# Holding back the context's gathered expert rows while the latents' pairs are selected and their weight table is built

## Chip, core and metric

The kernel runs on one core of one Trainium2 chip. The metric is device time in microseconds (us). All inputs lie in HBM when the kernel starts, and the whole computation, both layers of it, is one program on that core.

## What is computed

The reference runs two layers over 512 latent tokens and 256 context tokens, each a vector of 1024 numbers. A layer is a mixer (differential attention, a chunked MLP, a Fourier mix, gated and merged) and after it a retrieval of experts (PEER): each token picks 16 expert pairs in each of 8 heads, 128 experts in all, out of 16384.

```python
for l in range(DEPTH):                      # DEPTH = 2
    h = modulate(rmsnorm(x, norm1_g[l]), ...)          # latents
    hc = modulate(rmsnorm(xc, norm1_g[l]), ...)        # context
    ...
    x = x + mod[:, 2] * mixer_merge(...)    # attention reads kc, vc of hc too
...
def peer_ffn(h, w_q, sub_keys, u_tab, v_tab):
    ...
        q = rms_unit((t @ w_q).reshape(T, PEER_HEADS, 2, PEER_HALF))
        s = jnp.einsum('thpc,hpkc->thpk', q, sub_keys).astype(F32)
        s1, i1 = lax.top_k(s[:, :, 0], PEER_TOPK)
        s2, i2 = lax.top_k(s[:, :, 1], PEER_TOPK)
        ...
        top_s, pos = lax.top_k(cand_s, PEER_TOPK)
        idx = jnp.take_along_axis(cand_i, pos, axis=-1)
        g = jax.nn.softmax(top_s, axis=-1)
        act = jax.nn.gelu(jnp.einsum('td,thkd->thk', t, u_tab[idx]).astype(F32), approximate=False)
        return jnp.einsum('thk,thkd->td', (g * act).astype(t.dtype), v_tab[idx])
```

The context goes through the experts in the first layer only: in the second it gives keys and values to the attention, and nothing of it is written out. So what the context's experts add in layer 0 is needed at the start of layer 1, where the keys and values of the context are projected.

## The kernel before

**Two ways through the experts.** The latents of layer 0 (all four blocks of 128 tokens) go through every expert: `dense_u` multiplies 128 tiles of the table u with the tokens, `dense_v` multiplies the activations by a routing weight and then by 128 tiles of the table v. The weight is zero for an expert that a token didn't pick; the table of these weights is made by `gtable` (for each token one-hot rows `oa` and `ob`, and a matmul of the two into `px`, copied to `stg` and stored), from the indices `i1x`, `i2x` that `route2` selects (its one-hot masks are `oh`). The two context blocks of layer 0, `rc[0]` and `rc[1]`, go the other way: for each of a token's 128 experts, GpSimd issues an indirect DMA that gathers one u row for each of the 128 tokens (a tile `row` of 128x1024, 512 KB), and VectorE multiplies it with the token and sums up (L867); then the same with the v rows, each scaled and added to `acc` (L876). That is 128 u and 128 v rows for each block, 512 for the two. In layer 1 the last block of the latents goes that way too, with 256 rows.

**Who sets when rows are issued.** Rows have no place of their own in the program. Each group of three matmuls calls `pace()`, which adds the columns over 2.4 (nanoseconds of TensorE) to `owed`; at each 1700 of it, `step()` is called once. One step issues a gather and, LAG = 3 rows behind, uses a row that was gathered earlier. There are LAG + 1 = 4 row buffers, so a gather waits until the row four places ahead of it has been used. Each weight tile that is loaded takes 1800 off `owed` (`spend()`). The VectorE and GpSimd instructions thus stand between those of whatever work has called `pace()`. Queues run in the order written, on each engine.

**The order of the work.** Layer 0: mixer; routing of the context (its rows are queued then); norm and routing of the latents (`route1`, `route2`) and their weight table, with 54 of the 128 tiles of `dense_u` between as filling; then the dense stage, `dense_v` for each tile with the other tiles of `dense_u` between. Layer 1 begins with the Fourier mix and chunk MLP of the latents (`mix()`). Beside it runs `context()`: it waits for the sum of `rc[1]` or for the end of `mix()`, whichever comes first, then finishes the rows that are left one behind the other (`finish`, with no pacing), adds them to the context (`residual`: load `racc`, transpose in `tl`, L898 into `rx`, store `cfin`), and makes the normed context hH, hL (`norm`, L335), which the projections of the context in `qkv` need.

```python
            def context():
                while "summed" not in rc[1] and not mixed:
                    yield
                self.finish(rc[1])
                ...
                    for b, r in enumerate(rc):
                        self.residual(tmp, l - 1, self.cm, cin, b, r["accd"], 1)
                        yield
                    yield from self.norm(tmp, l, cin, CTX, 0, 1, ctx.parts)
```

Of the kernel before, what the change touches and what calls it, by code (L numbers as in the profile page):

```python
# [77 lines left out]
class Ker:  # L78
    def __init__(self, tc, a, es):
        self.tc, self.nc, self.a, self.es = tc, tc.nc, a, es  # L80
        self.uid, self.turn, self.banks = 0, False, PBANKS
        self.wp = self.wb = self.wr = None
        self.jobs, self.flight, self.owed, self.every = [], [], 0, STEPS[0][0]


    def pool(self, es, name, bufs=1, space=None, side=None):
# [738 lines left out]
        self.jobs.append({"l": l, "r": r, "tab": tab, "next": 0})  # L825

    def pace(self, cols):
        self.owed += cols / 2.4
        while self.owed >= self.every:
            self.owed -= self.every  # L830
            self.step()
# [167 lines left out]
    def layer(self, l, xin, cin, xfin, rin):  # L999
        nc, a, tc, two = self.nc, self.a, self.tc, self.two  # L1000
        last = l == DEPTH - 1
# [181 lines left out]
        def ahead(n):  # L1183
            while len(gSs) < n:
                c = order[len(gSs)]
                gSs[c] = self.dense_u(l, c, self.pp, up, dH, dL, "ps", self.banks["ps"])
                yield
        with ExitStack() as e:
            rp = self.pool(e, f"rp{l}")
            for b in range(4):  # L1190
                for n in ("i1", "i2", "g"):
                    if n not in rx[b]:
                        rx[b][n] = rp.tile([P, P], F32, name=f"{n}x{l}_{b}")
            gt, normed = [], []

            def routing():
                with ExitStack() as e2:
                    tmp = self.pool(e2, f"rn{l}")
                    yield from self.norm(tmp, l, xm, SEQ, 1, 0, lambda k: (dH[:, k, :], dL[:, k, :]), r1)
                    normed.append(True)  # L1200
                with ExitStack() as e2:
                    tmp = self.pool(e2, f"rt{l}")
                    yield from self.route1(l, tmp, rp, SimpleNamespace(H=dH, L=dL, T=SEQ), (tmp, *PQB))
                with ExitStack() as e2:
                    tmp = self.pool(e2, f"nat{l}")
                    for b in range(NDB, 4):
                        self.natural(tmp, rx[b]["hnd"], dH, dL, b)
                gt.append(self.pool(e, f"gt{l}"))
                yield from self.route2(gt[0], list(range(NDB, 4)) + list(range(NDB)), rx, l)

            def table():
                for b in range(NDB):
                    while "done" not in rx[b]:
                        yield
                    yield from self.gtable(gt[0], b, rx[b], gd)

            def fill():
                while not normed:
                    yield
                yield from ahead(SPILL[l][0] + NGS - LEAD)  # L1220
            self.interleave((self.ada(*((l, range(10, 12)) if last else (l + 1, range(ADA))), None, "fl"), 4 * AN[l]),
                            (None if last else cr, CR2), (routing(), 1), (table(), 1), (fill(), FILL[l]))
        epp.close()

# [181 lines left out]
```

## Time and profile before

| what | us |
|---|---|
| runs | 4987.19, 4993.69, 11380.49; median 4993.69 |
| profiled execution, its own time | 4982.3 |
| span of its instructions | 4980.5 |
| PE (TensorE) busy | 4521.8 (91%) |
| DVE (VectorE) busy | 3366.8 (68%) |
| POOL (GpSimd) busy | 2029.4 (41%) |
| ACT (ScalarE) busy | 1910.4 (38%) |

The stages as they lie in the span: mixer of layer 0 to about 980; routing of the context and norm of the latents to about 1240; the latents' pair selection and weight table to about 1690; the dense stage from about 1760 to 2893; the mix of layer 1 from about 2920 to 3150; after it projections and attention to about 3700, then routing and table of layer 1 to about 4113, and its dense stage to the end. Busy times of engines lie beside one another; what counts for the time is which engine others wait for in a stage. The run of 11380.49 is a disturbed one.

### The profile page before, as it was taken

The numbers are of one execution on the slowest core, as the hardware profiler recorded it, in microseconds if no ns is written. First come the engines' busy times: TensorE is split into PE (matmuls) and PEld (weight loads), VectorE is DVE, ScalarE is ACT, GpSimd is POOL, SyncE is SP. The second block draws the span as 40 slices with busy tenths as digits, with TensorE's granted clock in tenths as the row PEclk, the third lists the DMA queues.
The fourth block names the chain that finished last, engine by engine and source line by source line (L and its number), as shares of the span: only waits on it lengthen the run. The fifth ranks groups of instructions, "written<-read, shape, count | busy, mean of one in ns | idle before, by whom it ended". The sixth has DMA issues, their size and how long they took to land.

```text
span 4980.5 us, 65298 instructions
## 1 busy us (share of the span) xinstructions
PE 4521.8 (91%) x23501; PEld 3851.7 (77%) x23501; DVE 3366.8 (68%) x6818; ACT 1910.4 (38%) x3201; POOL 2029.4 (41%) x1246
## 2 busy tenths in 40 slices
PE   7899988789789899999899989989897899999998
PEld 4787777667667788877778767767787788999998
DVE  3115485868888667766777874457459976777787
ACT  2222444322578522222222233334334783333332
POOL 1011012335655565655556420111225665555531
PEclk9999999989999999999999999999999899999999
DMA  4442245556567889988889886333536668888986
GB/s 167 144 135 68 92 134 167 170 174 217 200 223 247 297 285 318 318 290 273 272 294 303 306 267 204 101 96 110 170 92 192 214 241 297 293 289 301 302 287 228
DMA packets 447508, 1092.84 MB, mean 219 GB/s; under 512 B 37200, under 2 KB 193744, under 8 KB 440016
## 3 DMA queue, kind: packets, MB, share of 16 engines
q1 hardware_dynamic: 336592, 685.97, 42.2%
q0 software_dynamic: 110592, 402.70, 23.6%
q8 instruction: 185, 3.03, 0.2%
q14 instruction: 139, 1.14, 0.1%
HBM read 970.04 MB, written 118.49 MB: 219 GB/s over the span
## 4 chain that ended last, share of the span: by engine, by line
PE 57%; DVE 15%; issue 8%; DMA 8%; POOL 5%; ACT 4%; SPq 0%; POOLq 0%; DVEq 0%; ACTq 0%
PE du L113 6%; PE du L115 5%; PE du L114 5%; PE da L114 5%; PE da L113 5%; PE da L115 5%; PE ps L113 3%; PE ps L114 3%; PE ps L115 3%; DMA row<-in_u_dram,idxc 2%; POOL row L848 2%; PE px L929 2%; DVE row L867 2%; PE px L113 2%; PE px L115 2%
## 5 line engine op out<-in xcount | busy, mean ns | idle before, releaser
L109 POOL TENSOR_TENSOR wL<-wraw,wH 128x1024 fp32r<-128x1024 f32 x291 | 714.9, 2458 | 1138.9 <-ACT wH L102 1053.4
L102 ACT ACTIVATE wH<-wraw 128x1024 fp32r<-128x1024 f32 x460 | 486.7, 1059 | 1155.2 <-PE du L114 319.5
L113 PE MATMUL du<-dH,wH 128*128 128x512 f32 (+1 forms) x2048 | 781.5, 382 | 64.5 <-DVE da L990 45.5
L115 PE MATMUL du<-dH,wL 128*128 128x512 f32 (+1 forms) x2048 | 774.1, 378 | 43.8 <-DVE wL L109 22.6
L114 PE MATMUL du<-dL,wH 128*128 128x512 f32 (+1 forms) x2048 | 769.5, 376 | 6.5 <-DVE dL L335 6.5
L113 PE MATMUL da<-AH,vH 128*128 128x512 f32 (+1 forms) x1792 | 647.3, 363 | 7.8 <-ACT AH L102 7.8
L114 PE MATMUL da<-AL,vH 128*128 128x512 f32 (+1 forms) x1792 | 651.1, 363 | 0.7 <-DVE AL L109 0.6
L115 PE MATMUL da<-AH,vL 128*128 128x512 f32 (+1 forms) x1792 | 650.5, 363 | 0.0
L867 DVE SCALAR_TENSOR_TENSOR row<-row,hn 128x1024 f32<-128x1024 f32 x384 | 508.6, 1345 | 103.6 <-DMA row<-in_u_dram,idxc 89.8
L102 ACT ACTIVATE vH<-vr 128x1024 fp32r<-128x1024 f32 x256 | 271.7, 1062 | 779.6 <-PE da L114 550.1
L876 DVE SCALAR_TENSOR_TENSOR acc<-row,dots,acc 128x1024 f32<-128x1024 f32 x381 | 501.2, 1315 | 7.6 <-DMA row<-in_v_dram,idxc 3.7
L113 PEld LDWEIGHTS du<-dH,wH 128*128 128x128 f32 x2048 | 399.9, 195 | 123.1 <-DVE da L990 56.2
L848 POOL DMA_INDIRECT row<-in_v_dram,idxc x256 | 327.8, 1280 | 406.1 <-DVE acc L876 354.7
L115 PEld LDWEIGHTS du<-dH,wL 128*128 128x128 f32 x2048 | 400.2, 195 | 94.2 <-DVE wL L109 27.1
L848 POOL DMA_INDIRECT row<-in_u_dram,idxc x256 | 334.2, 1305 | 324.1 <-DVE row L867 228.4
L114 PEld LDWEIGHTS du<-dL,wH 128*128 128x128 f32 x2048 | 400.0, 195 | 47.5 <-DVE dL L335 9.0
L109 DVE TENSOR_TENSOR wL<-wraw,wH 128x1024 fp32r<-128x1024 f32 x169 | 220.8, 1307 | 269.0 <-ACT wH L102 256.4
L990 DVE TENSOR_TENSOR da<-d,da 128x512 f32<-128x512 f32 (+1 forms) x254 | 158.1, 622 | 333.3 <-PE d L115 332.8
L113 PEld LDWEIGHTS da<-AH,vH 128*128 128x128 f32 x1792 | 337.8, 189 | 43.9 <-ACT AH L102 8.5
L114 PEld LDWEIGHTS da<-AL,vH 128*128 128x128 f32 x1792 | 338.0, 189 | 37.7 <-DVE AL L109 2.4
L115 PEld LDWEIGHTS da<-AH,vL 128*128 128x128 f32 x1792 | 338.0, 189 | 35.3
L109 DVE TENSOR_TENSOR vL<-vr,vH 128x1024 fp32r<-128x1024 f32 x256 | 326.2, 1274 | 50.9 <-ACT vH L102 49.2
(385 smaller groups left out, 9441.9 us busy)
## 6 DMA issues: line engine op xcount, KB each, us to landing
wraw<-in_uT_dram SPq DMA_DIRECT2D x256, 512.0 KB, 4.6
vr<-in_v_dram SPq DMA_DIRECT2D x256, 512.0 KB, 6.1
wraw<-in_wt_dram SPq DMA_DIRECT2D x204, 512.0 KB, 3.7
gd<-stg SPq DMA_DIRECT2D x56, 1024.0 KB, 5.4
araw<-in_wada_dram SPq DMA_DIRECT2D x96, 512.0 KB, 4.4
gt<-gd SPq DMA_DIRECT2D x16, 2048.0 KB, 18.0
gt<-gd SPq DMA_DIRECT2D x16, 1536.0 KB, 12.4
gatex<-g SPq DMA_DIRECT2D x48, 256.0 KB, 2.1
```

The lines of the kernel that those rows point to most:

```text
L102: nc.scalar.activation(H, src, AF.Copy)
L109: e.tensor_tensor(L, src, H.bitcast(F32), op=ALU.subtract)
L113: nc.tensor.matmul(out, aH, bH, start=start, stop=False)
L114: nc.tensor.matmul(out, aH, bL, start=False, stop=False)
L115: nc.tensor.matmul(out, aL, bH, start=False, stop=stop)
L848: nc.gpsimd.indirect_dma_start(out=row, out_offset=None, in_=self.a[f"{job['tab']}{job['l']}"], in_offset=bass.IndirectOffsetOnAxis(ap=r[" ...
L867: nc.vector.scalar_tensor_tensor(row, row, 1.0, job["hn"], op0=ALU.mult, op1=ALU.mult, accum_out=dots[:, j:j + 1])
L876: nc.vector.scalar_tensor_tensor(job["acc"], row, dots[:, j:j + 1], job["acc"], op0=ALU.mult, op1=ALU.add)
L929: nc.tensor.matmul(gp[:, j * P:(j + 1) * P], ob[:, j, :], oa[:, j, :], start=True, stop=True)
L990: add = nc.vector.tensor_tensor(acc7, s[:, :TD], acc7, op=ALU.add)
```

## The change

A flag `held` makes `pace()` do nothing. It is set ahead of the latents' pair selection in layer 0 and taken back when the weight table has been built. In between, `owed` doesn't grow and no `step()` is called: no row is issued and none is used. No work is taken away; the rows that don't stand there stand later. `STEPS`, `LAG` and all else are as before, and layer 1 sets no flag.

```diff
@@ Ker.__init__
         self.jobs, self.flight, self.owed, self.every = [], [], 0, STEPS[0][0]
+        self.held = False
@@ Ker.pace
     def pace(self, cols):
+        if self.held:
+            return
         self.owed += cols / 2.4
         while self.owed >= self.every:
@@ Ker.layer, routing() and table()
                         self.natural(tmp, rx[b]["hnd"], dH, dL, b)
+                self.held = not last
                 gt.append(self.pool(e, f"gt{l}"))
                 yield from self.route2(gt[0], list(range(NDB, 4)) + list(range(NDB)), rx, l)
@@
                     yield from self.gtable(gt[0], b, rx[b], gd)
+                self.held = False
```

Three lines are put in ahead of most of the code, so L867, L876, L848, L897 and L898 of the kernel before are L870, L879, L851, L900 and L901 of the changed one.

GpSimd's queue in the table stage, the kernel before (`row<-in_u_dram` are the gathers, `oh` the masks of the pair selection, `ob` the one-hot rows of the table, `wL` the low part of a dense weight tile):

```order
L848 DMA row_11468<-in_u_dram,idxc_0_94 128x1024
L926 TENSOR_SCALAR ob_11526<-iota,sT_10796 128x128
L848 DMA row_11585<-in_u_dram,idxc_0_94 128x1024
L786 TENSOR_TENSOR oh_11490<-oh_11490,pIF_10906 128x2048
L926 TENSOR_SCALAR ob_11598<-iota,sT_10796 128x128
L926 TENSOR_SCALAR ob_11627<-iota,sT_10796 128x128
L848 DMA row_11677<-in_u_dram,idxc_0_94 128x1024
L786 TENSOR_TENSOR oh_11591<-oh_11591,pIF_10906 128x2048
```

The same queue in the changed kernel, from the last gather ahead of the stage on:

```order
L851 DMA row_14252<-in_u_dram,idxc_0_94 128x1024
L110 TENSOR_TENSOR wL_10592<-wraw_10589,wH_10591 128x1024
L110 TENSOR_TENSOR wL_10680<-wraw_10677,wH_10679 128x1024
L787 TENSOR_TENSOR oh_10673<-oh_10673,pIF_10413 128x2048
L787 TENSOR_TENSOR oh_10718<-oh_10718,pIF_10413 128x2048
L110 TENSOR_TENSOR wL_10832<-wraw_10829,wH_10831 128x1024
L749 CAST pIF_10870<-pI_8762 128x256
L929 TENSOR_SCALAR ob_10772<-iota,sT_10766 128x128
```

The gathers are gone from between the masks and the one-hot rows. Counted over the two orders on VectorE, 104 rows have been used at the first multiplication of the dense stage in the kernel before, and 41 in the changed one: 63 rows stand later.

VectorE's queue at the end of the context's rows in the mix of layer 1, the kernel before (`pq` is Fourier work, `acc` the sum of the context's v rows, `rx` the residual):

```order
L876 SCALAR_TENSOR_TENSOR acc_20735<-row_24142,dots_17818,acc_20735 128x1024
L876 SCALAR_TENSOR_TENSOR acc_20735<-row_24158,dots_17818,acc_20735 128x1024
L109 TENSOR_TENSOR wL_24432<-wraw_24429,wH_24431 128x1024
L109 TENSOR_TENSOR pq_24013<-ps_24154,pq_24012 128x256
L109 TENSOR_TENSOR pq_24015<-ps_24182,pq_24014 128x256
L109 TENSOR_TENSOR wL_24518<-wraw_24515,wH_24517 128x1024
L109 TENSOR_TENSOR pq_24015<-ps_24235,pq_24014 128x256
L898 SCALAR_TENSOR_TENSOR rx_24256<-tl_24258,mod_72,rx_24256 128x128 x2
```

The same queue in the changed kernel, from the last two instructions of the chunk MLP (`ct`) on:

```order
L641 SCALAR_TENSOR_TENSOR ct_24717<-tl_24712,sm_76,cbs_24270 128x512
L645 TENSOR_TENSOR ct_24717<-ct_24717,cu_24532 128x512
L879 SCALAR_TENSOR_TENSOR acc_21944<-row_24655,dots_19024,acc_21944 128x1024
L879 SCALAR_TENSOR_TENSOR acc_21944<-row_24693,dots_19024,acc_21944 128x1024
L879 SCALAR_TENSOR_TENSOR acc_21944<-row_24705,dots_19024,acc_21944 128x1024
...
L879 SCALAR_TENSOR_TENSOR acc_21944<-row_24809,dots_19024,acc_21944 128x1024
L879 SCALAR_TENSOR_TENSOR acc_21944<-row_24812,dots_19024,acc_21944 128x1024
L901 SCALAR_TENSOR_TENSOR rx_24825<-tl_24827,mod_72,rx_24825 128x128 x4
L901 SCALAR_TENSOR_TENSOR rx_24825<-tl_24836,mod_72,rx_24825 128x128 x4
```

Before, the last row stands in the middle of the Fourier mix, and mix work follows it. Now 34 rows stand in one piece behind the whole mix (with one small instruction of the projections among them), and the residual behind these. Between the last dense tile of layer 0 and the end of the chunk MLP stand 54 rows, where 25 stood in all.

TensorE's queue at the same place, the kernel before (`tl` with `ident` are the transposes of the residual, `ps` Fourier products):

```order
L115 MATMUL ps_24235<-bH_24172,z_23494 128x256
L897 MATMUL tl_24258<-ident,racc_24254 128x128
L113 MATMUL ps_24277<-bH_24172,z_23493 128x256
L114 MATMUL ps_24277<-bL_24173,z_23493 128x256
L115 MATMUL ps_24277<-bH_24172,z_23494 128x256
```

And in the changed kernel (`ps_25012` is the end of a projection of the latents, `tl` the residual, L294 and L305 the norm of the context, `px_25013` its projection):

```order
L115 MATMUL ps_25012<-wL_25060,hH_22991 128x512
L116 MATMUL ps_25012<-wH_25059,hL_22992 128x512
L900 MATMUL tl_24827<-ident,racc_24823 128x128 x4
L900 MATMUL tl_24836<-ident,racc_24823 128x128 x4
L900 MATMUL tl_24850<-ident,racc_24846 128x128 x4
L900 MATMUL tl_24859<-ident,racc_24846 128x128 x4
L294 MATMUL tl_24908<-onescol,nr_24869 128x1 x2
L305 MATMUL tl_24930<-dg_24927,ones 128x128 x2
L114 MATMUL px_25013<-wH_25017,hH_22993 128x512
```

Before, the transposes stand between Fourier products of the mix. Now residual, norm and the first projection of the context stand in one piece, behind the last product of the chunk MLP and 44 matmuls of a latent projection, with nothing between.

## Rows read from the trace of the kernel before

**Rows 1.** The page, part 1: busy time of each engine.

```profile
PE 4521.8 (91%) x23501; PEld 3851.7 (77%) x23501; DVE 3366.8 (68%) x6818; ACT 1910.4 (38%) x3201; POOL 2029.4 (41%) x1246
```

**Rows 2.** Stretch, length; PE, PEld, DVE, ACT, POOL busy; clock, DMA share, GB/s.

```profile
1240.00:1680.00 440.00, 377.48 (x2071) 297.56 (x2070) 378.76 (x883) 314.07 (x612) 256.92 (x152) 0.95 0.67 230
1800.00:2100.00 300.00, 300.00 (x1325) 248.40 (x1324) 224.88 (x237) 86.51 (x111) 181.66 (x127) 1.00 0.92 314
2200.00:2500.00 300.00, 272.20 (x1154) 219.64 (x1153) 209.22 (x296) 77.10 (x96) 167.65 (x108) 0.98 0.83 272
2900.00:2920.00 20.00, 3.27 (x14) 3.22 (x15) 14.24 (x31) 2.52 (x4) 6.04 (x5) 0.58 0.84 289
2920.00:3140.00 220.00, 207.62 (x1089) 164.14 (x1088) 109.23 (x183) 77.33 (x121) 16.27 (x15) 0.96 0.65 211
```

**Rows 3.** What TensorE waited for in the table stage: us, times, longest.

```profile
PE tl L906 <- DVE i2x L787: 14.7, 2, 9.7
PE px L929 <- DVE ob L926: 8.5, 7, 2.1
PE du L115 <- DVE wL L109: 7.6, 3, 6.3
...
PE du L115 <- POOL wL L109: 7.0, 4, 3.8
```

**Rows 4.** The row instructions of the table stage: duration ns min/median/max.

```profile
L867 DVE SCALAR_TENSOR_TENSOR row<-row,hn x59: 1204/1216/3385, 1240.7 to 1679.1; 128x1024 f32<-128x1024 f32 x59
L848 POOL DMA_INDIRECT row<-in_u_dram,idxc x58: 937/1284/1931, 1242.2 to 1672.7; - x58
```

**Rows 5.** The chain of waits through the table stage, shares by line.

```profile
by line: issue 12.6%; PE px L929 10.7%; DVE ob L926 7.6%; PE du L115 7.2%; ACT stg L930 7.0%; PE du L113 6.8%; PE du L114 6.7%; DVE oa L918 5.2%; DVE row L867 4.3%; POOL oh L786 4.2%; POOL ob L926 3.2%; POOL wL L109 2.9%; ACT ob L924 2.9%; 
```

**Rows 6.** The dense stage, 2200 to 2500, u rows: waits, and the rows themselves.

```profile
PE du L113 <- DVE da L990: 25.8, 12, 4.6
...
DVE row L867 <- DMA row<-in_u_dram,idxc: 36.2, 19, 5.1
...
L867 DVE SCALAR_TENSOR_TENSOR row<-row,hn x90: 1207/1219/3503, 2200.4 to 2499.1; 128x1024 f32<-128x1024 f32 x90
```

**Rows 7.** VectorE in time at the end of the context's rows: start, length.

```profile
3033.36 1.28 DVE L876 SCALAR_TENSOR_TENSOR acc<-row,dots,acc 128x1024 f32<-128x1024 f32 x1 [0.59 <-DMA row<-in_v_dram,idxc]
3035.69 1.34 DVE L876 SCALAR_TENSOR_TENSOR acc<-row,dots,acc 128x1024 f32<-128x1024 f32 x1 [1.04 <-DMA row<-in_v_dram,idxc]
...
3038.37 1.28 DVE L876 SCALAR_TENSOR_TENSOR acc<-row,dots,acc 128x1024 f32<-128x1024 f32 x1 [1.02 <-DMA row<-in_v_dram,idxc]
...
3040.71 2.60 DVE L876 SCALAR_TENSOR_TENSOR acc<-row,dots,acc 128x1024 f32<-128x1024 f32 x2
```

**Rows 8.** GpSimd in time at the same place: three of its last gathers for the context.

```profile
3030.40 1.87 POOL L848 DMA_INDIRECT row<-in_v_dram,idxc  x1 [0.59 <-DVE acc L876]
...
3033.89 1.58 POOL L848 DMA_INDIRECT row<-in_v_dram,idxc  x1 [0.30 <-issue]
3035.77 0.94 POOL L848 DMA_INDIRECT row<-in_v_dram,idxc  x1 [0.30 <-issue]
```

**Rows 9.** From the last row to the normed context: stores and loads, residual, norm.

```profile
3043.34 0.33 SPq L878 DMA_DIRECT2D accdc<-acc  x1
...
L898 DVE SCALAR_TENSOR_TENSOR rx<-tl,mod,rx x16: 347/350/353, 3053.3 to 3066.4; 128x128 f32<-128x128 f32 x16
...
3066.77 0.56 SPq L899 DMA_DIRECT2D cfin<-rx  x1
...
L335 DVE SCALAR_TENSOR_TENSOR hL<-nt,mod,hH x8: 479/484/488, 3094.5 to 3110.5; 128x256 fp32r<-128x256 f32 x8
```

**Rows 10.** Landing of the gathers from 2990 to 3045, beside the mix.

```profile
DMA to landing us min/median/max: 4.4/5.7/8.7
```

**Rows 11.** A row's multiplication in the dense stage, and GpSimd beside it.

```profile
2320.63 3.33 DVE L867 SCALAR_TENSOR_TENSOR row<-row,hn 128x1024 f32<-128x1024 f32 x1 [0.90 <-DMA row<-in_u_dram,idxc]
...
2320.49 2.39 POOL L109 TENSOR_TENSOR wL<-wraw,wH 128x1024 fp32r<-128x1024 f32 x1 [0.77 <-ACT wH L102]
```

## Prediction

> **What bounds the kernel now.** I read the busy times first: TensorE is busy for 91% of the span, VectorE for 68%, GpSimd for 41% [rows 1]. A change that takes no work from TensorE can therefore gain only in stretches where TensorE stands still, and loses wherever it makes a new one. So the second view is the busy time by stretches [rows 2]. The reader is to see how unlike they are. Where v rows of the context run beside the dense stage (1800 to 2100), TensorE has no idle time at all, with the DMA engines at 0.92. Where u rows run there (2200 to 2500), it is idle for 300 - 272.2 = 27.8 us. In the table stage, from which the change takes the rows, it is idle for 440 - 377.5 = 62.5 us, with VectorE busy for 379 of 440. In the mix of layer 1 it is idle for 220 - 207.6 = 12.4 us, and VectorE and the DMA engines have room (109 of 220; 0.65).
>
> Third come the waits of TensorE in the table stage [rows 3]. It waits for VectorE's pair selection (14.7), one-hot rows (8.5) and weight split (7.6): 30.8 us for VectorE, and 7.0 for GpSimd's split. The rows themselves are named in none of these; they stand ahead of what is named, in the same queues. The chain of waits says the same from the other side: VectorE's row multiplications hold 4.3% of those 440 us, 19 us [rows 5].
>
> Last come the end of the context's rows in layer 1 and what follows on it, in order of time [rows 7 to 9], since the order of the changed kernel puts them in another place: the last 34 rows, residual, norm and projection of the context in one piece behind the mix.
>
> **Table stage, a gain.** 63 rows stand elsewhere. The trace has 59 multiplications there at a median of 1.216 us and 58 gathers at 1.284 [rows 4]: VectorE loses 59 x 1.216 = 72 us of its 379, GpSimd 58 x 1.284 = 74 us of its 257. TensorE's work of 377 us stays, so no more than its idle 62.5 us can come back, and not all of that: part of it is start-up of each table matmul and ScalarE's work, which no row delays. Lower bound: the 19 us for which rows hold the chain, less what takes their place there, since one-hot rows and stage copies (7.6% and 7.0%) run close behind [rows 5]; I take 10. Upper bound: 50. Between them I take the waits for VectorE, 31 us, as the row nearest to the question: with a fifth of its work gone, VectorE should be ahead of the table matmuls. **-31** (-50 to -10).
>
> **Dense stage, a loss.** As many u rows more run beside dense tiles, in the same small clusters ahead of the add into `da`. In the stretch with u rows 90 of them go with 27.8 us of idle TensorE, 25.8 of it a wait for that add [rows 2, 6]. 63 x 27.8 / 90 = **+20**. The bounds: 10, if half of those waits would be there without rows; 28, if the first tiles of the stage, which have less slack, take half as much again. In return as many v rows leave the end of the stage, which cost nothing [rows 2].
>
> **The mix of layer 1.** Ahead of the burst 54 rows run where 25 ran. The 29 more of 0.524 MB are 15.2 MB over some 220 us, 69 GB/s on 211: 280, less than the 314 at which TensorE was never idle [rows 2]. On VectorE they are 29 x 1.28 = 37 us [rows 7] in a stretch with 111 free. The context's residual and norm leave the stretch, and can take some of its 12.4 us of idle TensorE along. I take **0** (-6 to +13: all of the context's share, or as much idle again as is there now).
>
> **The burst, a loss.** What hid the last rows and the context's norm was the mix. Now nothing of the mix is left behind them: on TensorE only 44 matmuls of a latent projection stand ahead of the first transpose of the residual. At 300 us / 1325 = 0.226 us each [rows 2] that is 10 us of cover. Rows: four are in their buffers, 4 x 1.28 = 5 us [rows 7]. Each of the other 30 goes round a ring of four buffers: gather, landing, multiplication, next gather. From the start of the gather at 3030.40 to its use at 3035.69, which waited for the landing, it took 5.29 us [rows 7, 8]; with the use of 1.28 and GpSimd's 0.30 ahead of a gather that makes 6.9 us for four rows, 1.7 each. GpSimd alone gave (3035.77 - 3030.40) / 3 = 1.79 for one. 30 x 1.7 = 51, so 56 us in all. Bounds: 1.28 for each of 34, 44 us, if VectorE is the limit; and (3040.71 - 3033.36) / 3 = 2.45 for each, 83 us, which is what uses at the end of the context's rows had, with weight loads and Fourier work between [rows 7].
>
> **What follows on the burst.** The last sum goes out at 3043.34, the first normed tile is there at about 3094.5 + 0.9 = 3095.4 [rows 9]: 52 us, all hidden by the mix so far, of which sixteen residual steps of 0.35 us took 13 because of other work between. With the engines otherwise empty I take 48 (41 to 52). Nobody works meanwhile: TensorE's queue has the residual's transposes, two small norm products and the context's projection there, in this order, and everything of `qkv` and the attention is queued behind them. So 56 + 48 - 10 = **+94** (79 to 125). TensorE comes out of such a stop at a lower granted clock: at the boundary of the layers, busy for 3.27 of 20 us, it had 0.58 (between its two levels) [rows 2]. I put **+3** on the time until it is back (0 to 5).
>
> **What two pages would make of it.** A row's multiplication that ran beside GpSimd's split of a weight tile took 3.33 us where the median is 1.219, and the split 2.39 [rows 6, 11]. The Trainium skill, "SBUF — State Buffer", section "Who interferes with whom", says why: a VectorE instruction with two SBUF inputs and a GpSimd instruction that reads SBUF exclude each other. This trace agrees for this pair. The rule speaks for taking rows out of the table stage and against putting them beside the splits of the dense stage, where rows reach 3.5 us too [rows 4, 6]; both are in the terms above already, so the sum stays.
>
> For the ring of four buffers the landing decides, and rows show 4.4 us at least and 5.7 in the median [rows 10]. The Trainium skill, "DMA: Bandwidth & Descriptors", section "Anatomy of one DMA — SWDGE (gpsimd) path", gives about 2.0 us plus bytes over 436 GB/s, by which an estimate for 512 KB is 3.2 us. By that page VectorE would be the limit at 1.28 us a row, the burst 44 us and the sum 12 us lower. This trace has no gather as quick, so the rows stand.
>
> **The sum.** -31 + 20 + 0 + 94 + 3 = +86 on the profiled execution's 4982.3: 5068. That execution lies 11.4 us below the median of the runs and 4.9 below the lowest of the two that are undisturbed. I add 7 and forecast **5075 us**, 1.6% above the median of 4993.69. About 2% (100 us; slower from 5094, faster below 4894) is what a measurement of this kernel can tell from no change.
>
> **Rivals.**
> 1. *Slower: the burst goes at the pace of 2.45 us a row.* At the end of the mix the weight loads of the projection are fetched ahead, and gathers that share the DMA engines with them land late; the uses at 3033 to 3041 show three waits in a row for a landing [rows 7]. Then the burst is 83 us and the time 5075 + 27 = 5102, +2.2%. It decides from 2.25 us a row (19 us more). Against it: these gaps had other VectorE work between, and in a standstill weight loads stop once their buffers are full.
> 2. *Slower: the table stage gives little back.* The rows filled gaps in queues that wait for TensorE or ScalarE anyway, and the change doesn't free what it means to free. With 10 instead of 31 the time is 5096. For it: rows hold 4.3% of the chain only [rows 5]. Against it: VectorE is at 86% there and is what TensorE waits for most [rows 2, 3].
> 3. *Little loss.* The table stage gives 50, the burst runs at VectorE's pace (44) and what follows takes 41: -50 + 20 + 75 + 3 = +48, 5037; with the dense stage at 10 it is 5027. For it: residual and norm are alone on their engines.
> 4. *Faster by over 2%.* All idle time of the table stage and of the mix together is 75 us [rows 2]; even with no burst that is 1.5%. Nearly excluded.
>
> **How the numbers follow.** The forecast's case, all terms near their middle, between 5040 and 5093: 0.50. Rival 1: 0.22. Rival 2: 0.13. Rival 3: 0.13. Rival 4: 0.02. The forecast and rival 3 are within 2% (0.63); rivals 1 and 2 lie just above the line, so I leave 0.35 for slower and 0.63 for no difference. The range leaves out the lower half of rival 3 and the upper tail of rival 1, when its pace goes together with a small gain in the table stage (5102 + 21 = 5123): 5025 to 5118. All the cases but rival 4 are a loss; whether it passes 2% is nearly open.
>
> **What will show it.** In the table stage of the changed kernel TensorE's busy time stays at about 377 us in some 410, and the waits for VectorE's `ob`, `i2x` and weight splits are mostly gone. In the first tiles of the dense stage u rows run for some 200 us longer, with TensorE waiting for the add into `da`. At about 3150 us (some 10 us earlier if these two terms hold) VectorE has 34 uses of `acc` in a row, 1.7 us apart, waiting for landings, and TensorE is empty for about 94 us, which ends with `px` of the context's projection. Wrong would make it: other projections of TensorE that run ahead of the transposes; rows that pile up in the mix until VectorE holds TensorE there; or a table stage whose waits move to ScalarE's `stg` and ends no earlier.

## Result: 1.7% slower, inside the range

The changed kernel takes 5071.18 us (median of four runs, 5068.46 to 5072.83), the kernel before 4990.98 beside it. The ratio is 1.017 (95% interval 1.0157 to 1.0183), where +1.6% was forecast, and under the 2% drawn as the line for "slower". One run of the kernel before (11380.49 us) is disturbed and left out of the ratio: against the median of the other three, 4988.27, the loss is 83 us, against the median of all four 80.

The busy time of each engine over the span is as before to within 1% [rows 1], since no work was added or taken away; the span is 88 us longer.

```profile
span 5068.8 us, 65325 instructions
...
PE 4532.9 (89%) x23501; PEld 3853.3 (76%) x23501; DVE 3384.8 (67%) x6818; ACT 1910.5 (38%) x3201; POOL 2019.6 (40%) x1246
```

The stretches, as in [rows 2]: the table stage, which ends at 1642 and not at 1673; the last dense tiles and the mix of layer 1; and the 100 us behind the mix.

```profile
1240.00:1640.00 400.00, 363.60 (x2044) 287.45 (x2043) 313.08 (x768) 310.14 (x608) 169.00 (x94) 0.97 0.49 174
2860.00:3140.00 280.00, 247.56 (x1269) 198.93 (x1267) 177.73 (x229) 82.32 (x122) 84.24 (x66) 0.95 0.78 262
3140.00:3240.00 100.00, 8.86 (x22) 3.84 (x20) 49.56 (x64) 3.11 (x8) 36.74 (x31) 0.52 0.62 205
```

In the last of them TensorE works for 9 of 100 us, with a granted clock of 0.52, near the lower of its two levels. That is the loss, and the three longest waits of TensorE from 3100 to 3300 name it:

```profile
PE tl L900 <- DMA racc<-accdc: 63.5, 1, 63.5
PE tl L294 <- DVE nr L283: 17.6, 1, 17.6
PE tl L900 <- DVE rx L901: 8.2, 15, 1.9
```

The first of these is the burst with the store and load of its sum, the second the norm's sums, the third the residual. Ahead of the sum's store VectorE does nothing but rows (and one instruction of 0.22 us); its view in time, as [rows 7], first and last of the burst and two from the middle:

```profile
3133.78 5.24 DVE L879 SCALAR_TENSOR_TENSOR acc<-row,dots,acc 128x1024 f32<-128x1024 f32 x4
3141.16 1.28 DVE L879 SCALAR_TENSOR_TENSOR acc<-row,dots,acc 128x1024 f32<-128x1024 f32 x1 [2.15 <-DMA row<-in_v_dram,idxc]
...
3152.64 1.28 DVE L879 SCALAR_TENSOR_TENSOR acc<-row,dots,acc 128x1024 f32<-128x1024 f32 x1 [0.90 <-DMA row<-in_v_dram,idxc]
...
3196.02 1.35 DVE L879 SCALAR_TENSOR_TENSOR acc<-row,dots,acc 128x1024 f32<-128x1024 f32 x1 [0.31 <-DMA row<-in_v_dram,idxc]
```

34 rows from 3133.78 to 3197.37 are 63.6 us, 1.87 for each. The row instructions of the burst and the landing of its gathers, as [rows 4, 10]:

```profile
L879 DVE SCALAR_TENSOR_TENSOR acc<-row,dots,acc x34: 1280/1285/1627, 3133.8 to 3196.0; 128x1024 f32<-128x1024 f32 x34
...
DMA to landing us min/median/max: 4.6/5.5/6.5
```

A multiplication still takes 1.285 us. The rest goes into the round of gather, landing and use over four buffers: VectorE waits for landings 19 times in the burst, 18.5 us in all, and between its gathers GpSimd waits for a row to be used. No run here changes the number of buffers, so this is read from the waits and not tested. What follows, on TensorE and SyncE, as [rows 9]:

```profile
3139.89 0.39 PE L116 MATMUL ps<-wH,hL 128*128 128x512 f32 x1
3203.73 0.45 PE L900 MATMUL tl<-ident,racc 128*128 128x128 f32 x1 [63.46 <-DMA racc<-accdc]
...
3237.09 1.01 PE L294 MATMUL tl<-onescol,nr 128*128 128x1 f32 x4 [17.64 <-DVE nr L283]
3241.14 1.20 PE L305 MATMUL tl<-dg,ones 128*128 128x128 f32 x4 [3.03 <-DVE dg L299]
3243.86 0.79 PE L114 MATMUL px<-wH,hH 128*128 128x512 f32 x1 [1.53 <-ACT hH L335]
3244.46 0.63 PE L115 MATMUL px<-wL,hH 128*128 128x512 f32 x1
```

```profile
3197.40 0.33 SPq L881 DMA_DIRECT2D accdc<-acc  x1
```

From the store of the sum (3197.40) to the first projection of the context (3243.86) it is 46.5 us. TensorE's last matmul ahead of the stop begins at 3139.89 and ends at about 3140.3, so it stands, but for transposes, for 103.6 us. The gains and losses lie where landmarks of the two traces fall against one another. A landmark is the first or last instruction of a line, and its lag is its time in the changed kernel less that in the kernel before, in us. For the adds into `da` (the sum of the dense stage) it is read from these two lines, the kernel before first:

```profile
L990 DVE TENSOR_TENSOR da<-d,da x127: 678/692/692, 1764.2 to 2896.5; 128x512 f32<-128x512 f32 x127
```

```profile
L993 DVE TENSOR_TENSOR da<-d,da x127: 677/691/692, 1725.1 to 2884.7; 128x512 f32<-128x512 f32 x127
```

| landmark | lag |
|---|---|
| routing of the context, about 960, ahead of the change | +6.0 |
| first transpose of the weight table | +0.8 |
| last `stg` of the weight table | -31.0 |
| first add into `da` | -39.1 |
| last add into `da` | -11.8 |
| first normed latents of layer 1 | -10.3 |
| last chunk MLP product | -15.2 |
| first softmax of layer 1's attention | +88.4 |
| end of the span | +88.3 |

The first 6 us are none of the change: the instructions are the same there, and in the first 100 us this execution had a granted clock of 0.85, the profiled one of the kernel before 0.98. Without them the trace says +82, the runs 80 to 83.

### The profile page after: what moved, and what is told of

Read it like the earlier page. It is cut to its first block, busy times and chain, and to the rows that moved or that the text cites. A ratio compares the mean times of both kernels' runs of the same rounds, so it can differ in the third digit from the quotient of the medians.

```text
span 5068.8 us, 65325 instructions
## 1 busy us (share of the span) xinstructions
PE 4532.9 (89%) x23501; PEld 3853.3 (76%) x23501; DVE 3384.8 (67%) x6818; ACT 1910.5 (38%) x3201; POOL 2019.6 (40%) x1246
## 4 chain that ended last, share of the span: by engine, by line
PE 55%; DVE 16%; DMA 11%; issue 9%; POOL 4%; ACT 3%; SPq 0%; POOLq 0%; DVEq 0%; ACTq 0%
PE du L114 5%; PE du L115 5%; PE du L116 5%; PE da L115 5%; PE da L116 5%; PE da L114 5%; PE ps L114 3%; DMA row<-in_u_dram,idxc 3%; PE ps L116 3%; PE ps L115 3%; POOL row L851 2%; PE px L932 2%; DVE row L870 2%; PE px L114 2%; PE px L116 2%
## 5 line engine op out<-in xcount | busy, mean ns | idle before, releaser
L870 DVE SCALAR_TENSOR_TENSOR row<-row,hn 128x1024 f32<-128x1024 f32 x384 | 516.6, 1365 | 124.2 <-DMA row<-in_u_dram,idxc 112.4
L879 DVE SCALAR_TENSOR_TENSOR acc<-row,dots,acc 128x1024 f32<-128x1024 f32 x381 | 503.0, 1320 | 41.3 <-DMA row<-in_v_dram,idxc 37.3
L851 POOL DMA_INDIRECT row<-in_v_dram,idxc x256 | 328.5, 1283 | 421.6 <-DVE acc L879 366.7
L851 POOL DMA_INDIRECT row<-in_u_dram,idxc x256 | 333.0, 1301 | 322.8 <-DVE row L870 250.2
L114 PEld LDWEIGHTS da<-AH,vH 128*128 128x128 f32 x1792 | 336.8, 188 | 41.1 <-ACT AH L103 6.1
```

Of the source, the lines that this page charges most:

```text
L114: nc.tensor.matmul(out, aH, bH, start=start, stop=False)
L851: nc.gpsimd.indirect_dma_start(out=row, out_offset=None, in_=self.a[f"{job['tab']}{job['l']}"], in_offset=bass.IndirectOffsetOnAxis(ap=r[" ...
L870: nc.vector.scalar_tensor_tensor(row, row, 1.0, job["hn"], op0=ALU.mult, op1=ALU.mult, accum_out=dots[:, j:j + 1])
L879: nc.vector.scalar_tensor_tensor(job["acc"], row, dots[:, j:j + 1], job["acc"], op0=ALU.mult, op1=ALU.add)
```

## Experiments

Ratios are to runs of the kernel before on the same chip, with the 95% interval. Lags are landmarks as in the table, against the same profiled execution of the kernel before. They carry the scatter of both executions: in the run with cover but without the hold, whose instructions up to layer 1 are those of the kernel before, the table stage took 5 us longer than there, and the dense stage 7.

**The stop without the hold.** The flag is set for the last 27 dense tiles instead, where v rows cost TensorE nothing [rows 2].

```diff
-                self.held = not last
                 gt.append(self.pool(e, f"gt{l}"))
...
                 for c in range(NK):
+                    self.held = not last and c >= NK - 27
                     room[0] += not self.spilled(l, c)
...
+                self.held = False
                 known = not last and TD == SEQ
```

> No hold in the table stage; instead pace() is held for the last 27 tiles of the dense stage of layer 0, where v rows cost TensorE nothing. The row count at the start of the dense stage is that of the kernel before (104 used); 32 rows stand in one piece behind the mix of layer 1 (34 in the changed kernel). Theory (the loss is the stop at the end of the mix: burst, then residual and norm with nothing beside them): 32 x 1.87 us, the pace in the changed kernel's burst, + 47 - 10 = 97 us over the kernel before, less up to 10 from fewer rows beside the last dense tiles and the boundary: 5075 to 5090. Rival (the loss comes from the rows that the hold puts into the first dense tiles, and rows behind the mix are hidden somehow): 4985 to 5010.

Measured: 1.0181 (1.0164 to 1.0198), +90 us, within the 87 to 97 of the theory's sum; the median of 5072.98 lies just under its 5075, since the kernel before took 4980.57 beside it. Table and dense stage keep their times (lags -1.2 at the last `stg`, -0.7 at the last add into `da`), and the attention begins 91.9 us late. The waits of TensorE from 3100 to 3300:

```profile
PE tl L900 <- DMA racc<-accdc: 59.1, 1, 59.1
PE tl L294 <- DVE nr L283: 16.5, 1, 16.5
PE tl L900 <- DVE rx L901: 9.5, 15, 3.3
```

They are those of the changed kernel. So the stop alone makes a loss of this size, without the hold in the table stage; the rival falls.

**The table stage alone.** The 63 u rows are left out of the computation.

```diff
                 r["dots"] = gp.tile([P, P], F32, tag="dots", name=self.nm("dots"), bufs=2)
+                nc.vector.memset(r["dots"], 0.0)
...
                 self.held = False
+                if not last:
+                    self.jobs[0]["next"] += 63
```

> As the changed kernel, but the 63 u rows that it puts off are left out altogether (not gathered, not multiplied; their dot products stay zero), so the dense stage and layer 1 carry the same rows as in the kernel before. Theory: the gain of the table stage and of the way into the dense stage, 37 + 8 us in the trace, stays: 4940 to 4955. Rival (what the table stage gains is given back at the start of the dense stage, since TensorE is the limit there anyway): 4970 to 4990.

Measured: 0.9927 (0.9910 to 0.9945), -36 us. Lags: -37.9 at the last `stg`, -43.5 at the first add, -37.7 at the last one, -43.4 at the attention. What the table stage gains is kept to the end.

**Rows caught up in the dense stage, with the hold and without.**

```diff
-STEPS = ((1700, 1700, 1700), (1700, 1700, 1700))
+STEPS = ((1700, 1700, 1460), (1700, 1700, 1700))
```

> As the changed kernel, but the dense stage of layer 0 calls for a row at each 1460 of owed time, not 1700, so that the 63 rows are caught up there: 26 rows stand behind the first dense output add, 25 in the kernel before, and none behind the mix. Theory: gain of the table stage (-45), cost of 63 more u rows in the dense stage (+27), no stop in layer 1, nothing for rows that follow one another more closely beside v tiles: 4965 to 4980, a little faster than before. Rival (a denser row stream, with the DMA engines at 0.92 already, makes TensorE wait in the dense stage): 5000 to 5040.

> The kernel before with only the pace in the dense stage of layer 0 changed to 1460: no hold, and all rows of the context are used before the end of the dense stage. It prices the denser row stream alone. Theory: 4980 to 4995, no change, the rows that cross the boundary now lie a little earlier. Rival (denser rows cost TensorE time): 5010 to 5040.

Measured: 1.0081 (1.0064 to 1.0098) with the hold, 1.0098 (1.0079 to 1.0117) without. Both times (medians 5021.93 and 5026.43) lie in the rivals' ranges: here the theory of an almost free denser stream fell. Between the first and the last add into `da` the kernel before gets 63 us later by the pace alone (-4.9 to +58.1), the one with the hold 83 (-42.3 to +41.1). Why is seen in the v rows from 1800 to 2100. First the stretch at 1460 without the hold, as [rows 2]:

```profile
1800.00:2100.00 300.00, 283.42 (x1211) 230.79 (x1210) 257.74 (x231) 82.74 (x102) 190.98 (x130) 0.98 0.92 317
```

Then the groups of row instructions there (busy us, mean ns, idle time ahead), in that kernel and, in the fence behind it, in the kernel before:

```profile
L876 DVE SCALAR_TENSOR_TENSOR acc<-row,dots,acc 128x1024 f32<-128x1024 f32 x110 | 171.8, 1562 | 22.6 <-DMA row<-in_v_dram,idxc 22.2
```

```profile
L876 DVE SCALAR_TENSOR_TENSOR acc<-row,dots,acc 128x1024 f32<-128x1024 f32 x104 | 133.1, 1280 | 0.3 <-DMA row<-in_v_dram,idxc 0.3
```

And the same rows at 1460 by min/median/max:

```profile
L876 DVE SCALAR_TENSOR_TENSOR acc<-row,dots,acc x110: 1267/1274/3925, 1800.3 to 2098.0; 128x1024 f32<-128x1024 f32 x110
```

Only six more rows were used in these 300 us, but they cost VectorE 39 us more: the mean of a row goes from 1280 to 1562 ns, its median stays, and the longest takes 3925. Besides, VectorE waits 22 us for landings (0.3 before), and TensorE, which had no idle time here, stands for 16.6 us, all but 0.1 of it a wait for the add into `da`. The longest row, and the weight split on GpSimd beside it:

```profile
1874.55 3.92 DVE L876 SCALAR_TENSOR_TENSOR acc<-row,dots,acc 128x1024 f32<-128x1024 f32 x1
...
1874.97 2.41 POOL L109 TENSOR_TENSOR wL<-wraw,wH 128x1024 fp32r<-128x1024 f32 x1
```

In these 300 us 18 of the rows take more than 1.5 us, and each of the 18 overlaps such a split; of the 92 shorter ones one does. At 1700 the rows fell into the gaps between the splits: three of 103 touch one, and none is stretched. By the Trainium skill, "SBUF — State Buffer", section "Who interferes with whom", a VectorE instruction with two SBUF inputs and a GpSimd instruction that reads SBUF contend for a pair of ports that is locked, not shared. The trace agrees: the stretched rows reach about a row's own 1.27 us and a split's 2.4 together.

**Rows paced faster in the mix.** The change with 900, and with 1300, at the start of layer 1.

```diff
-STEPS = ((1700, 1700, 1700), (1700, 1700, 1700))
+STEPS = ((1700, 1700, 1700), (900, 1700, 1700))
```

> As the changed kernel, with the pace at the start of layer 1 raised (a row at each 900 of owed time, not 1700). All 88 rows that are left behind the dense stage then stand among the instructions of the mix, the last of them ahead of the chunk MLP's gating, and none behind the mix; table and dense stage are those of the changed kernel. Theory (the loss of the changed kernel is the stop at the end of the mix, about 97 us, and VectorE has room in the mix): the stop is gone; -41 for table stage and entry, +27 for u rows in the dense stage, and 0 to 30 for rows that the ring of four buffers (1.87 us each) can't deliver in time: 4985 less 14, plus 0 to 30, so 0.995 to 1.004 of the kernel before. Rival, after what a denser stream did to the dense stage (63 rows closer together cost 60 to 80 us there): VectorE's queue holds the mix up by as much, 1.010 to 1.015.

> As the changed kernel, with the pace at the start of layer 1 at 1300: 17 rows stand in one piece behind the mix, half of the 34. Theory (the stop is 1.87 us for each row behind the mix, and 47 for residual and norm, less 10 of cover, whatever stands ahead): 17 x 1.87 = 32 us less than the changed kernel, which was 1.017 to 1.018: 1.010 to 1.012 of the kernel before, with a standstill of TensorE of some 72 us. Rival (the rows that now stand closer together in the mix cost there what the burst saves): 1.016 to 1.020.

Measured: 1.0092 (1.0074 to 1.0109) and 1.0125 (1.0106 to 1.0144), each between the ranges of its theory and its rival. With 900 it is just under the rival's: the long wait for `racc` shrinks to 7.2 us, but the mix is held up. Its stretches:

```profile
2940.00:3060.00 120.00, 113.57 (x658) 90.28 (x656) 71.89 (x84) 38.97 (x64) 43.44 (x35) 0.99 0.89 312
3060.00:3160.00 100.00, 73.65 (x305) 59.20 (x305) 72.38 (x80) 22.98 (x29) 47.00 (x38) 0.88 0.87 303
...
3180.00:3200.00 20.00, 1.63 (x7) 1.57 (x8) 5.57 (x22) 3.33 (x8) 0.00 (x0) 0.53 0.29 92
```

TensorE is idle for 26 of 100 us while rows pile up from 3060, with the DMA engines at 0.87, and still stands for most of 20 us in the norm of the context, which comes so late that little of the mix is left beside it. With 1300 the wait for `racc` falls from 63.5 to 34.5 us, 29 for 17 rows fewer behind the mix, about what 1.87 a row says. But the mix, which got 5 us shorter in the changed kernel, gets 13 longer here (lag -12.8 at the first normed latents, +0.2 at the last chunk MLP product), so 18 us are given back. The theory's mechanism holds, and the mix, for which it had no price, takes more than half of what the burst saves.

**Half of the hold.** Two kernels: the hold until the pair selection has been written out, with the mix at 900; and the hold from there on.

```diff
                 yield from self.route2(gt[0], list(range(NDB, 4)) + list(range(NDB)), rx, l)
+                self.held = False
...
                     yield from self.gtable(gt[0], b, rx[b], gd)
-                self.held = False
```

```diff
-                self.held = not last
                 gt.append(self.pool(e, f"gt{l}"))
                 yield from self.route2(gt[0], list(range(NDB, 4)) + list(range(NDB)), rx, l)
+                self.held = not last
```

> As the run with the mix paced at 900, but the hold ends with the pair selection; beside the rest of the weight table rows run again. 52 rows are put off instead of 63, 77 are left behind the dense stage, none behind the mix. Theory (the rows cost the table stage about 0.65 us each, wherever they stand in it): gain of the table stage 52/63 of 41 = 34, cost in the dense stage 52/63 of 27 = 22, mix 0 to 20: 0.997 to 1.002 of the kernel before. Rival (rows cost most while VectorE is busy without a gap, in the pair selection): the whole 41 stays, 0.994 to 0.998.

> As the changed kernel, but the hold begins when the pair selection has been written out, so 14 rows are put off instead of 63; 39 are left behind the dense stage (25 before), all of them beside the mix, the last one at nearly the same place of the mix as before. Theory: a gain of 14 x 0.65 = 9 us in the table stage, a cost of 14 x 0.34 = 5 in the dense stage, no stop: 0.997 to 1.001 of the kernel before. Rival (the gain of the hold comes from the pair selection alone): 1.000 to 1.003.

Measured: 1.0052 (1.0036 to 1.0069) and 1.0013 (1.0000 to 1.0025). From the first transpose of the table to its last `stg`, the first gains 31 us (-4.1 to -35.5), as much as the whole hold (32); the second loses 3 (+0.8 to +3.6). So the gain of the table stage comes with the rows of the pair selection, as the rival had it, and not evenly from all rows. On the way into the dense stage, from the last `stg` to the first add into `da`, it is the other way round: the first gains nothing (-35.5 to -33.7), the second 8 us (+3.6 to -4.3), as much as the whole hold there.

Why the pair selection? From its first mask product on GpSimd to the last index on VectorE it takes 308 us in the kernel before and 184 in the changed one, of which VectorE is busy for 272 and 179 (the third of the busy times in these stretches, the kernel before first):

```profile
1269.00:1577.00 308.00, 257.76 (x1410) 202.87 (x1409) 272.34 (x636) 223.98 (x441) 191.09 (x109) 0.94 0.63 218
```

```profile
1262.00:1446.00 184.00, 155.89 (x844) 122.40 (x843) 179.09 (x437) 134.53 (x263) 92.21 (x47) 0.93 0.45 160
```

VectorE is busy nearly without a gap only once the rows are gone. Before, it also waited some 20 us for the masks on GpSimd, whose queue had the gathers between them; with the hold 1.8 us of that are left (the kernel before, then the changed one):

```profile
DVE i1x L787 <- POOL oh L786: 10.2, 2, 6.2
DVE i2x L787 <- POOL oh L786: 9.4, 2, 4.8
```

```profile
DVE i2x L788 <- POOL oh L787: 1.8, 1, 1.8
```

Every run here holds back multiplications and gathers together, so how much of the gain belongs to VectorE and how much to GpSimd's queue stays open. As a whole the first run is slower than either expectation, since the mix takes 28 us of it back (-5.4 at the first normed latents, +23.0 at the attention). The second lies in the rival's range, with an interval that reaches into the theory's. With 14 rows put off it lost 22 us in the dense stage of its profiled execution, as much as the first with 52, which no price per row explains; its runs scatter from 4979 to 5003 us, and that stays open.

**Cover for the stop.** The context's projections are written behind those of the latents, with eight weight tiles loaded and split a second time; once with the hold, once without.

```diff
-    self.interleave((self.qkv(tmp, l, both, PE3[l]), 1), (g0 if last else None, 0.6))
+    self.interleave((self.qkv2(tmp, l, both, PE3[l]) if last else self.qkv(tmp, l, both, PE3[l]), 1), (g0 if last else None, 0.6))
...
+    def qkv2(self, tmp, l, ss, e="pool"):
+        yield from self.qkv(tmp, l, ss[:1], e)
+        nc, a, s = self.nc, self.a, ss[1]
+        g = tmp.tile([P, 2, 64], F32, tag="gk", name=self.nm("gk"), bufs=1)
+        nc.sync.dma_start(g, a["kg"][l])
+        acc, = yield from self.projN(l, W_K, ss[1:], e)
+        self.qknorm(tmp, acc, g[:, 0, :], s.lat, *s.k)
+        acc, = yield from self.projN(l, W_V, ss[1:], e)
+        for b, o in enumerate(acc):
+            self.split(s.v[0][:, b, :], s.v[1][:, b, :], o)
+        yield
```

> As the changed kernel, with hold, 88 rows left and 34 of them behind the mix; but in layer 1 the projections of the context (keys, values) are written after all projections of the latents instead of sharing each weight tile with them. Eight weight tiles are loaded and split a second time. On TensorE 236 matmuls now stand between the chunk MLP and the residual's transposes (44 before), and 268 instructions between the first transpose and the first projection of the context (20 before). Theory (the loss is the missing cover, and nothing of the rows' work itself): (236 - 44 + 268 - 20) x 0.226 = 99 us more cover for a stop of about 97 us, so most of it is gone; -41 + 27 remain, and 0 to 20 for the extra loads and for VectorE's split of weights and qk-norm behind rows: 0.997 to 1.002 of the kernel before. Rival (VectorE's and the DMA engines' work for the rows holds up the projections of the latents as well, so cover on TensorE doesn't help): 1.010 to 1.017.

> The kernel before with the same order of projections in layer 1 and no hold: the price of the second load and split of eight weight tiles, and of the other order, alone. Theory: TensorE has the same matmuls, the DMA engines stand at a quarter there: 0.998 to 1.003 of the kernel before. If it is faster than the run with the hold, the hold isn't worth its cost even where the stop is covered; by -41 + 27 the hold should be faster than this by 5 to 25 us.

Measured: 1.0129 (1.0115 to 1.0144) with the hold, 1.0011 (0.9996 to 1.0027) without. The extra loads are about free. With the hold some 20 us come back, of the 75 to 100 that the expectation asked for: the time lies in the rival's range, and the hold is some 55 us slower than the same order without it, where 5 to 25 faster was expected. The two stretches behind the mix, and the longest waits of TensorE from 2880 to 3450 that belong to the second:

```profile
3140.00:3200.00 60.00, 49.98 (x200) 38.97 (x199) 46.76 (x49) 15.16 (x19) 39.74 (x31) 0.91 0.87 310
3200.00:3260.00 60.00, 12.86 (x35) 6.94 (x33) 31.82 (x74) 4.39 (x9) 12.03 (x7) 0.56 0.44 140
```

```profile
PE tl L294 <- DVE nr L283: 16.6, 1, 16.6
PE tl L912 <- DMA racc<-accdc: 14.9, 1, 14.9
...
PE tl L912 <- DVE rx L913: 12.6, 15, 6.4
```

While the burst runs TensorE is busy now (50 of 60 us), so cover does work, and the rival's reason is not what happened; the projections that were counted on for the second half stand behind the residual's transposes and the norm's products in TensorE's queue, and wait with them. Counting instructions between two places was the mistake: what stands behind a waiting instruction covers nothing.

**The two parts of the stop, and the dense stage alone.** Left out of the computation: 30 of the 34 v rows behind the mix; and, in another kernel, 63 v rows at the end of the dense stage.

```diff
+                self.jobs[0]["next"] = P - 1
                 self.finish(rc[1])
```

```diff
+                if not last:
+                    self.jobs[0]["next"] += 63
                 known = not last and TD == SEQ
```

> As the changed kernel, but 30 of the 34 v rows that stand in one piece behind the mix are left out (not gathered, not added); four stay, then residual, norm and projection of the context as in the changed kernel. Theory (the stop has two parts that add up, 64 us for the burst and 47 for what follows on it, with 10 us of cover): TensorE still stands for some 40 us behind the mix; 30 x 1.87 = 56 us less than the changed kernel's 1.017 to 1.018, so 1.005 to 1.008 of the kernel before. Rival (the stop is one of weight loads or of the clock that rows only accompany): 1.012 to 1.017.

> As the changed kernel, but 63 v rows are left out when the dense stage of layer 0 ends, so that 25 are left for layer 1 as in the kernel before, with the last one at the same place of the mix. Table stage and dense stage are those of the changed kernel, 63 more u rows in the dense stage among it. Beside the run that left out 63 u rows ahead of the dense stage (0.9927), the difference is those u rows in the dense stage alone. Theory (27 us in the landmarks of the trace, of which 6 came without them): 20 us, so 0.9965 to 0.998 of the kernel before, and faster than it. Rival, after the run that put off only 14 rows and still lost 22 us in the dense stage (a cost of how rows lie against tiles, not of their number): the dense stage costs nothing or twice as much here, below 0.995 or above 1.000.

Measured: 1.0054 (1.0034 to 1.0074), 58 us under the changed kernel for 30 rows, 1.93 for each, so the burst adds up as expected. What stays of the stop is the second part:

```profile
PE tl L294 <- DVE nr L283: 16.8, 1, 16.8
PE tl L900 <- DVE rx L901: 10.1, 15, 3.9
PE tl L900 <- DMA racc<-accdc: 4.9, 1, 4.9
```

And 0.9948 (0.9932 to 0.9964) for the other: the point lies just inside the rival's range (below 0.995), and the interval ends just short of the theory's 0.9965. Hold and u rows in the dense stage together, without the stop, are a gain of 26 us. Against the run without the 63 u rows that leaves 0.0021 x 4985 = 10 us for them, and from the ends of the intervals anything from -6 to 27. So the times don't decide between nothing and the theory's 20. The traces are sharper: from the first to the last add into `da`, six kernels with the 63 u rows there (the changed one, this run, both faster paces of the mix, the hold with cover, and the run without a burst) take 1155 to 1168 us, four without them (the kernel before, the late hold, the run without the u rows, and cover without the hold) 1132 to 1139. The means are 26 us apart.

## Why the prediction held, term by term

- **Table stage, -31.** Measured -31.8 from the first transpose of the table to its last `stg`, and kept (the run with rows left out). That it hit the number is in part luck. The term was the 30.8 us of three waits for VectorE [rows 3], and half of them stayed, though they were to be mostly gone:

```profile
PE du L116 <- DVE wL L110: 9.5, 3, 4.6
PE px L932 <- DVE ob L929: 5.3, 4, 2.2
...
PE tl L909 <- DVE i2x L788: 1.0, 1, 1.0
```

  That is 15.8 us. The waits for `i2x` went (14.7 to 1.0), those for one-hot rows and weight splits in the main not, and the 7.0 for GpSimd's split, which the term left out, went as well. The gain comes with the rows of the pair selection. Two pieces outside the stage as it was drawn were missing: 5 us ahead of it (+6.0 to +0.8) and 8 on the way into the dense stage. In all -45.
- **Dense stage, +20.** Measured +27.3, at the upper bound, and 26 between the means of the kernels with and without the u rows; TensorE's waits for the add into `da` between 1765 and 2880 grew from 34.4 to 54.5 us, as the term said (the kernel before, then the changed one):

```profile
PE du L113 <- DVE da L990: 34.4, 15, 4.6
```

```profile
PE du L114 <- DVE da L993: 54.5, 21, 5.2
```

- **The mix, 0.** Measured -5 (-10.3 at the first normed latents, -15.2 at the last chunk MLP product): 54 rows did no harm there. That the context's norm left the mix is not shown to be the gain, since the mix got 4 to 9 us shorter, too, in three runs where norm and rows stand in it much as before (those without the 63 u rows, without the 63 v rows, and with cover alone).
- **The burst and what follows, +94, and the clock, +3.** Measured +103.6 in the lags, from the last chunk MLP product to the attention, for both terms together (97). The burst was sized a little low (56; 63.6 measured, 1.87 a row for 1.7), what follows a little high (48; 46.5), and the cover too high: 10 us of matmuls were there, but the burst began when they were already under way, and 6.5 of them counted. The bounds had a slip: 44, 41 and -10 make 75, not 79. Of the clock: it is granted at 0.58 from 3244 to 3250 us, near the lower of its two levels, and at 1.00 from 3250 to 3256; a matmul begins every 0.43 us for about the first 12 behind the stop, then every 0.23: 2.4 us.
- **Rivals.** A burst at 2.45 us a row did not come: 1.87. A table stage that gives nothing back neither. Less loss needed a burst at 1.28 a row; a round of landing, use and issue, 5.5 + 1.285 + 0.3 us for four buffers, makes 1.77 a row and leaves no room for that. The estimate of 3.2 us for a gather, worked out from the Trainium skill, "DMA: Bandwidth & Descriptors", section "Anatomy of one DMA — SWDGE (gpsimd) path", is not borne out here: no gather of the burst landed in less than 4.6.
- **The sum** was near because its errors offset, which is luck: 14 us more gain around the table and 5 in the mix, against 7 more in the dense stage, 7 in the stop and 1.5 at the boundary of the layers. The 7 us added for the scatter of executions came as the 6 ahead of the change.

No run here that does the whole computation is faster than the kernel before. What a row costs depends on where it stands: nothing that shows beside v tiles and beside the mix, as long as the rows come no more closely than the ring and the gaps of GpSimd's splits allow; more beside u tiles and beside the pair selection; and 1.87 us, its whole round, where nothing runs beside it.

## What to carry to other kernels

Before work is put off from a stage with no slack, count what the later stages can take at the pace that they have, and look for the place where the rest is flushed: 34 leftovers there undid the gain twice over, since the flush brought the serial steps behind it out of hiding as well. Cover on an in-order engine is only what stands ahead of the first instruction that waits. And a stream of gathered rows that costs nothing at one pace can cost a lot at a slightly denser one, once its VectorE work falls beside GpSimd's, so a catch-up has to be priced by itself.

## What was not expected

A pace of 1460 instead of 1700 for gathered rows beside the dense tiles costs about 48 us (1.0098), though the same rows are used: rows of 1.28 us are stretched to 1.56 in the mean and 3.9 at most, the long ones beside a weight split on GpSimd. And what the hold gains before the dense stage is uneven: the rows beside the pair selection cost some 30 us, the last 14 about 8, and these on the way into the dense stage.
